# Moving the gate branch and the norm of q into the channel tiles of a recurrence

## The chip, the cores and the metric

The kernel runs on one core of a Trainium2 chip, in one launch. The metric is the device time of one execution in microseconds. The kernel before takes 1188.15 us, the median of three runs (1186.73 to 1192.13).

## What is computed

One layer of a diffusion backbone: 1024 latent tokens with a context of 256, 1024 channels, float32. Of the reference, cut to what matters here (`x` and `ctx` are normed and modulated into `h` and `hc` first):

```
q, k, v, xr, gr = split(h @ w_in)          # q 512 columns, k 128, v 128, xr 512, gr 512
q = apply_rope_2d(rmsnorm(q, q_norm_g))    # per head of 64, 8 heads
k = apply_rope_2d(rmsnorm(k, k_norm_g))    # 2 heads
attn = windowed_attention_with_context(q, k, v, k_c, v_c, sink)
xc = centred_depthwise_conv(xr)            # width 4; context and latents apart
for d in (forward, backward):              # RG-LRU, 512 channels
    r = sigmoid(block_diag(xc, w_r[d]));  i = sigmoid(block_diag(xc, w_i[d]))
    log_a = -8 * r * softplus(-lam[d]);   a = exp(log_a)
    h_sum += scan(a, sqrt(-expm1(2 * log_a)) * i * xc)
y = concat([attn, h_sum * gelu(gr)]) @ w_out
x = x + g1 * y
x = x + g2 * expert_choice_moe(modulate(rmsnorm(x)))    # 16 experts, SwiGLU, 128 tokens each
```

## The kernel before

All products with large weights are done in float32r in three parts: a float32 weight or activation is split into a high half (`whi`, `hh`) by a copy on ScalarE and a low half (`wlo`, `hl`) by a subtraction on VectorE, and a product is high x high + high x low + low x high. A weight of 256 columns is fetched by SyncE into one of two raw buffers (`load_raw`, `win`), and `split_w` makes the halves (L241 on ScalarE, L243 on VectorE); three of each can be held.

The part that the change touches lies between the keys and values and the attention, 175 to 326 us:

- **Recurrence** (`lru_tile`, channel tiles t = 3, 2, 1, 0 of 128 channels; 1280 time steps in a row). TensorE multiplies the convolved input with two gates in two directions (`pgatec` for the context, `pgate` for the latents). ScalarE makes tanh of the four, then `a` = exp and one more tanh for each direction, then two square roots. VectorE multiplies `i` with the input (L503), the factor with the root (L507, L508), scans both directions (L511, L513, L515) and adds them into `xr` (L517).
- **Projection of q** (`proj`, `pproj`): 2 groups g of 256 columns by 8 blocks b of 128 tokens, 24 matmuls each; ScalarE copies each into `QB[b]`. Five of these 16 steps stand behind each of the first three tiles and one behind the last.
- **Gate branch**, behind all four tiles: for each channel tile 48 matmuls (`pgr`), gelu on ScalarE (`ge`), and the product with `xr` on VectorE (L585).
- **Keys** (`k_stack`): each pair of key heads is copied twice, transposed on TensorE, and split into `kh` and `kl`.
- **Norm and rotation of q** (`norm_rope`), behind the gate branch: squares on ScalarE (L404), sums on VectorE (L406), the reciprocal root on GpSimd (`rstd_of`, L147 and L149), then on VectorE the product with it (L408), two cross terms (L418), the cosine term (L420) and the sum (L421). It needs both groups of a block.
- **Attention** follows: `q_stack` transposes and splits a block of q (`qst`), `scores` multiplies it with the keys, `load_wout` splits the eight halves of the output weight (`woh`, `wol`), `oproj` is the output projection (`py`).

PSUM has two buffers of 1024 columns (tag S: gates, `pgr`, scores), one each of O0 and O1 (512 columns: `pproj` and `pgatec` in turn) and two for transposes (T). The framework that builds the program does not keep the written order: it makes one list of instructions for each engine ahead of time, from the dependencies and its own estimates, and each engine then runs its list strictly in order, waiting where an input is late or a buffer is not free. `act` is the exception: activations that go through it keep their written order among themselves (`tc.issue_after`, which orders an instruction behind another). ScalarE holds one set of functions at a time; a change of set is an ACT_TABLE_LOAD in its list. Exp and tanh share a set, sqrt has another, gelu another, which holds tanh as well: in the lists no load stands between gelu and a tanh that follows it.

Of the kernel before, what the change touches and what calls it, by code (L numbers as in the profile page):

```python
# [13 lines left out]
OP = mybir.AluOpType  # L14
# [34 lines left out]
def _body(tc, nc, A, out, dbg, top):  # L49
# [35 lines left out]
    def act(*a, **kw):  # L85
        """an activation whose table set matters: these keep their order on the engine"""
        if last_act[0] is None:
            i = nc.scalar.activation(*a, **kw)
        else:
            with tc.issue_after(last_act[0].ins):  # L90
                i = nc.scalar.activation(*a, **kw)  # L91
        last_act[0] = i
        return i
# [4 lines left out]
    def warm(n, after=None):  # L98
        """keeps the tensor engine's clock up while it waits"""
        p = pS("warm")  # L100
        for _ in range(n):
            with tc.issue_after(after.ins) if after is not None else nullcontext():
                after = nc.tensor.matmul(p[:, 0:128], ident, ident, start=True, stop=True)

# [47 lines left out]
    # softplus(-lam) = max(-lam, 0) + log1p(exp(-|lam|)); log1p(e) = 2 atanh(e / (2 + e))  # L152
# [22 lines left out]
    # sigmoid(z + b) = (1 + tanh(z / 2 + b / 2)) / 2  # L175
# [18 lines left out]
    def ada_chunk(n):  # L194
        """[4 groups x (16 rows of c, 16 of c_ctx), 512] of columns n*512.., in SBUF"""
        po = pO("pada")
        for q in range(2):
            for half in range(2):
                w = paw.tile([128, 4, 256], F32, name="wada")
                c0 = n * 512 + q * 256  # L200
                nc.sync.dma_start(w, w_ada[half * 512:(half + 1) * 512, c0:c0 + 256].rearrange("(k p) c -> p k c", p=128))
                for j in range(4):
                    nc.tensor.matmul(po[32 * j:32 * j + 32, q * 256:(q + 1) * 256], cst[:, half * 4 + j, :], w[:, j, :],  # L203
                                     start=(half == 0), stop=(half == 1),
                                     skip_group_check=True, tile_position=(0, 32 * j))
        ev = paw.tile([128, 512], F32, name="adaev", bufs=1)
        nc.vector.tensor_copy(ev, po)
        return ev

    ada_ev = {}  # L210
    gcol = const.tile([128, 40], F32, name="gcol")       # g1, sh2, sc2, g2, (1 + sc2) * norm2_g

    def ada_col(n):
        """half of one of g1, sh2, sc2, g2 as columns; the half before is finished first"""
# [40 lines left out]
    def projT(hi, lo, segs):  # L255
        """channel rows: [128 channels, tokens]"""
        for k in range(KT):
            for w, which in ((hi, (0, 1)), (lo, (0,))):
                for i in which:
                    for o, sg in segs:  # L260
                        h, c0, n = SEG[sg][i], SEG[sg][2], SEG[sg][3]
                        mm(o, w[:, k, :], h[:, k, c0:c0 + n], k == 0 and w is hi and i == 0, k == KT - 1 and w is lo)

# [1 line left out]
    AB = const.tile([128, 2, 8, 2], F32, name="ab")      # (scale, shift), k tile, (lat, ctx)  # L265
    a0 = pool(S_a0, "a0", 2)
    a0x = pool(S_a0, "a0x", 6)
    xT = a0.tile([128, KT, 768], F32, name="xT", bufs=1)      # [ctx 256 | lat 512]
# [24 lines left out]
    def ada_half(h):  # L293
        """scale and shift of half of the channels"""
# [64 lines left out]
    XR14 = pxr.tile([128, 4, NT + 6], F32, name="xr")    # slots 1 to 4; slot 0  # L359
    XR0 = pxr.tile([128, NT + 6], F32, name="xr0")  # L360
    XR = [XR0] + [XR14[:, i] for i in range(4)]
    XC0, XL0 = 0, NCTX + 3                               # [2 | ctx | 1 | 2 | lat | 1]
# [9 lines left out]
    def rope_tables(nm, after=None):  # L372
        """weights of the norm; cos and sin tables with them folded in"""
# [16 lines left out]
    def proj(wg, tt):  # L390
        """token rows: [128 tokens, 256 columns]"""
# [9 lines left out]
    def norm_rope(x, nh, b, tabs_):  # L401
        """x: [128, nh, 64], in place; b: latent block, or None (no rope)"""
# [54 lines left out]
    def gate_weights(t):  # L457
        """block-diagonal [128, (gate, direction), 128] of the channel tile"""
# [8 lines left out]
    def conv(t):  # L467
        """into slot t + 1, whose input is used up"""
# [62 lines left out]
    # the router with the second norm's scale in its rows, and its shift's share as a row  # L531
# [13 lines left out]
    qsteps = [(g, b) for g in range(2) for b in range(NB)]  # L545
    for i, t in enumerate((3, 2, 1, 0)):
        lru_tile(t)
        for g, b in qsteps[5 * i:5 * i + 5]:
            if b == 0:
                wg = split_group(load_raw(g * 256))  # L550
            po = proj(wg, b + 2)
            nc.scalar.activation(QB[b][:, g * 256:(g + 1) * 256], po, AF.Copy)

    S_lru.close()

# [20 lines left out]
    with tc.tile_pool(name="grt", bufs=2, side="right", reuse_waits="tile") as pg_:  # L576
        for t in (3, 2, 1, 0):
            if t % 2:
                raw = load_raw(1280 + (t - 1) * 128)
            w0 = xr_weights(raw, t)  # L580
            lat = pS("pgr")
            projT(w0[0], w0[1], [(lat[:, 0:512], LAT0), (lat[:, 512:1024], LAT1)])
            ge = pg_.tile([128, S], F32, name="ge")
            act(ge, lat, AF.Gelu_apprx_tanh)
            nc.vector.tensor_tensor(XR[t + 1][:, 0:S], XR[t + 1][:, 0:S], ge, op=OP.mult)  # L585
            if t in (1, 0):
                k_stack(1 - t)
        for b in range(NB):
            norm_rope(QB[b].rearrange("p (h d) -> p h d", h=8), 8, b, qtab)
    tiny = const.tile([128, 1], F32, name="tiny")  # L590
    act(tiny, nsink[:, 0:1], AF.Exp)
# [15 lines left out]
    S_wo, S_wr, S_cs, S_att = (ExitStack() for _ in range(4))  # L607
    WO = []                                              # (hi, lo) of the attention's rows, of the recurrence's rows
# [27 lines left out]
    def q_stack(b):  # L636
        """[128 (hi, lo), head, 128]; heads 2i: (hi, lo), heads 2i + 1: (lo, hi)"""
# [11 lines left out]
    def scores(b, kv, i, qst):  # L649
        """heads kv * 4 + i and kv * 4 + 2 + i of 128 queries: negated scores, then their exponentials"""  # L650
# [5 lines left out]
        # keys: the window, then the context; for the last block the other way round  # L656
# [38 lines left out]
    def attn_out(b, kv, i, pe, ktiles, mx):  # L695
# [20 lines left out]
        # [(head pair, d), (head of the pair, query)]  # L716
        nc.scalar.activation(QB[b][:, kv * 256 + i * 128:kv * 256 + (i + 1) * 128], po, AF.Copy)

    y7 = QBQ[1].rearrange("p a b -> p (a b)")[:, 0:D]         # the last block's share of the recurrence, over queries used up

    def oproj(b, hh, part):
        """half of the columns of x + g1 * (mixed @ w_out); part 0: the recurrence's rows of w_out, 1: the attention's"""
# [95 lines left out]
    # ---- the 128 largest affinities of each expert: halves of blocks sorted on their own, then merged  # L818
# [3 lines left out]
    def resort(m, np_, steps=(64, 32, 16, 8, 4, 2, 1)):  # L822
        """bitonic rows sorted downwards"""
# [9 lines left out]
    def sort_blocks(b0, n):  # L833
        """n blocks from b0: rows (block, expert), sorted downwards"""
        q = n * 32
        f = 1 if n == 4 else 2                           # rows per block and expert
# [20 lines left out]
    def merge(a, b):  # L857
        """the 128 largest of two sorted rows: bitonic"""
# [29 lines left out]
    for u, (b, kv, i) in enumerate(units):  # L888
# [15 lines left out]
        if u == 3:  # L904
            XA = praw.tile([128, 2, D], F32, name="xa", tag="raw")     # residual stream of two blocks
            XB = praw.tile([128, 2, D], F32, name="xb", tag="raw")     # the same, normalised
            load_res(0)
            load_res(1)
# [28 lines left out]
    tri = prt.tile([128, 2, 128], BF, name="tri")        # tri[t', t] = t' <= t; ones  # L937
# [49 lines left out]
    POS = prt.tile([128, NB, NE], F32, name="pos")  # L987
    VAL = prt.tile([128, NB, NE, 4], BF, name="val")     # token row within its block, 3 parts of the affinity
    pd = pool(top, "moe", 2)
    # the threshold and how many of the ties at it are taken, as rows on every partition  # L990
# [3 lines left out]
    ge = rt.tile([128, NB, 2, NE], BF, name="ge")        # above the threshold; at it  # L994
# [13 lines left out]
    def prefix(m):  # L1008
        """inclusive count over the tokens before (block by block), per expert"""
# [43 lines left out]
    def load_chunk(key):  # L1053
        """the next 256 rows of a weight: per 128 of them what float32r holds, and the rest"""
# [44 lines left out]
    def split_x(src, first=False):  # L1099
        """the second norm's scale and shift on the way"""  # L1100
# [141 lines left out]
```

## Time and profile before

| | |
|---|---|
| median of three runs | 1188.15 us |
| the profiled execution, first to last instruction (span; all that the profile gives of its own time) | 1185.1 us |
| gates of tile 3 to the first score | 175.0 to 326.0 us |
| attention and what is between its blocks | 326 to about 575 us |
| experts | about 600 us to the end |
| TensorE, VectorE, ScalarE busy over the span | 92%, 80%, 67% |

The times of the profile count from the span's start. A busy time is what an engine spends in instructions; a matmul's record also covers its way through the array, so neighbouring records overlap, and the distance between two starts is the better measure of what one costs. The distance is also used for VectorE, whose records overlap by some 0.08 us. What ends an idle time is named behind the arrow.

### The profile page before, as it was taken

What the parts mean: (1) busy time and instruction counts of PE and PEld (TensorE: products, weight loads), DVE (VectorE), ACT (ScalarE), POOL (GpSimd) and SP (SyncE); (2) the same over time, 40 slices, a digit from 0 to 9 for tenths busy, and PEclk for the clock granted to TensorE, in tenths of its full rate; (3) what the DMA queues carried; (4) which work ended last, traced back from release to release, by engine and by line L of the source; (5) the groups of instructions that cost most, each with busy time, mean ns of one, the idle gap of its engine ahead of it and who ended that gap; (6) DMA issues with size and microseconds to landing.
All of it is one profiled execution on the core that took longest, in us unless ns stands there. A gap on an engine that the chain in (4) does not pass through costs nothing.

```text
span 1185.1 us, 17663 instructions
## 1 busy us (share of the span) xinstructions
PE 1091.7 (92%) x6481; PEld 876.0 (74%) x6481; DVE 946.1 (80%) x1577; ACT 792.2 (67%) x1159; POOL 148.6 (13%) x216
## 2 busy tenths in 40 slices
PE   3889999899799999999299999999999999999996
PEld 1568787667678888877187888888888888887774
DVE  3664557678795585867988999999999999989885
ACT  3652127666385666664268888888888888887873
POOL 2031110111300000000010111011111011110001
PEclk9999999899889999999699999999999999999998
DMA  9857720102141112116889999999999999999932
GB/s 293 293 175 239 236 64 5 40 1 69 37 108 54 55 54 89 55 54 235 334 300 342 342 382 399 382 391 388 384 381 402 383 394 380 383 377 355 359 101 36
DMA packets 97678, 277.14 MB, mean 234 GB/s; under 512 B 6060, under 2 KB 38088, under 8 KB 97592
## 3 DMA queue, kind: packets, MB, share of 16 engines
q1 hardware_dynamic: 90944, 255.87, 57.7%
q0 software_dynamic: 6000, 20.01, 6.8%
q8 instruction: 51, 0.84, 0.3%
q14 instruction: 35, 0.29, 0.1%
q10 hardware_dynamic: 648, 0.13, 0.1%
HBM read 259.21 MB, written 16.79 MB: 233 GB/s over the span
## 4 chain that ended last, share of the span: by engine, by line
PE 68%; DVE 12%; issue 7%; ACT 7%; DMA 4%; POOL 1%; SPq 0%; POOLq 0%; ACTq 0%; DVEq 0%
PE pu L96 14%; PE pg L96 14%; PE pd L96 13%; PE py L96 7%; PE pxr L96 3%; PE pav L713 3%; PE pscore L96 3%; PE pPT L703 3%; DVE mlo L1066 2%; DMA wada<-in_w_ada_dram 2%; ACT gate L91 2%; PE pproj L96 1%; PE pada L203 1%; PE pT L1107 1%; DVE gate L507 1%
## 5 line engine op out<-in xcount | busy, mean ns | idle before, releaser
L1066 DVE TENSOR_TENSOR mlo<-mraw,mhi 128x1024 fp32r<-128x1024 f32 x384 | 448.1, 1217 | 24.5 <-ACT mhi L1063 23.1
L1063 ACT ACTIVATE mhi<-mraw 128x1024 fp32r<-128x1024 f32 x384 | 397.7, 1064 | 75.4 <-PE pg L96 29.0
L96 PE MATMUL pg<-mlo,xsh 128*128 128x512 f32 x256 | 81.9, 401 | 1.4 <-DVE mlo L1066 1.4
L96 PE MATMUL pg<-mhi,xsh 128*128 128x512 f32 x256 | 80.9, 397 | 0.4 <-ACT xsh L1117 0.3
L96 PE MATMUL pu<-mlo,xsh 128*128 128x512 f32 x256 | 80.2, 394 | 0.8 <-DVE mlo L1066 0.5
L96 PE MATMUL pu<-mhi,xsh 128*128 128x512 f32 x256 | 80.8, 390 | 0.0
L96 PE MATMUL pg<-mhi,xsl 128*128 128x512 f32 x256 | 80.4, 395 | 0.0
L96 PE MATMUL pu<-mhi,xsl 128*128 128x512 f32 x256 | 79.1, 390 | 0.0
L96 PE MATMUL pd<-mlo,hdh 128*128 128x512 f32 x240 | 76.0, 398 | 2.4 <-DVE mlo L1066 2.4
L96 PE MATMUL pd<-mhi,hdh 128*128 128x512 f32 x240 | 76.3, 399 | 0.0
L96 PE MATMUL pd<-mhi,hdl 128*128 128x512 f32 x240 | 74.2, 390 | 0.0
L1156 POOL DMA_INDIRECT out_dram<-ys,idx x16 | 49.8, 3113 | 164.2 <-DVE ys L1154 164.2
L1094 POOL DMA_INDIRECT xs<-xh_dram,idx x16 | 21.4, 1335 | 373.0 <-ACT mhi L1063 317.2
L1116 ACT ACTIVATE xs<-pT,gcol 128x128 f32<-128x128 f32 x124 | 46.9, 462 | 26.2 <-PE pT L1107 26.2
L91 ACT ACTIVATE sc<-sc,mx 128x641 f32<-128x641 f32 (+1 forms) x64 | 50.9, 798 | 15.7 <-DVE mx L677 15.7
L96 PE MATMUL pproj<-wlo,hh 128*128 128x256 f32 x192 | 55.5, 289 | 4.4 <-DVE wlo L243 4.4
L677 DVE CUSTOM_DVE_ANT_0 sc<-pscore,kn,nsink 128x640 f32<-128x640 f32 (+1 forms) x64 | 53.4, 842 | 6.0 <-PE pscore L96 5.8
L96 PE MATMUL pproj<-whi,hh 128*128 128x256 f32 x192 | 57.5, 300 | 0.6 <-ACT gate L91 0.6
L709 ACT ACTIVATE pt<-pPT 128x512 f32<-128x512 f32 (+1 forms) x88 | 44.0, 533 | 18.7 <-PE pPT L703 17.6
L96 PEld LDWEIGHTS pu<-mlo,xsh 128*128 128x128 f32 x256 | 47.1, 188 | 12.6 <-DVE mlo L1066 3.5
L96 PEld LDWEIGHTS pg<-mhi,xsl 128*128 128x128 f32 x256 | 48.6, 190 | 10.6
L96 PEld LDWEIGHTS pg<-mlo,xsh 128*128 128x128 f32 x256 | 46.2, 189 | 13.5 <-DVE mlo L1066 4.6
(329 smaller groups left out, 2444.7 us busy)
## 6 DMA issues: line engine op xcount, KB each, us to landing
mraw<-in_w_gate_dram SPq DMA_DIRECT2D x64, 1024.0 KB, 7.6
mraw<-in_w_up_dram SPq DMA_DIRECT2D x64, 1024.0 KB, 9.3
mraw<-in_w_down_dram SPq DMA_DIRECT2D x63, 1024.0 KB, 9.0
wada<-in_w_ada_dram SPq DMA_DIRECT2D x48, 512.0 KB, 5.8
win<-in_w_in_dram SPq DMA_DIRECT2D x7, 1024.0 KB, 5.4
xt<-in_x_dram SPq DMA_DIRECT2D x8, 512.0 KB, 4.3
xa<-in_x_dram SPq DMA_DIRECT2D x8, 512.0 KB, 3.8
out_dram<-xa SPq DMA_DIRECT2D x8, 512.0 KB, 2.7
```

Source lines behind the costliest of these rows:

```text
L91: i = nc.scalar.activation(*a, **kw)
L96: nc.tensor.matmul(o, l, r, start=start, stop=stop)
L203: nc.tensor.matmul(po[32 * j:32 * j + 32, q * 256:(q + 1) * 256], cst[:, half * 4 + j, :], w[:, j, :], start=(half == 0), stop=(half == 1) ...
L677: nc.vector.tensor_tensor_reduce(out=sb[:, :ntot], in0=ps[:, n0:n0 + ntot], in1=mk, scale=-0.125, scalar=nsink[:, h:h + 1], op0=OP.add, op ...
L703: nc.tensor.transpose(p[:, 2 * j + s, :], pe[s][:, (j0 + j) * 128:(j0 + j + 1) * 128], ident)
L709: nc.scalar.activation(dst, src, AF.Copy)
L713: nc.tensor.matmul(po[s * 64:(s + 1) * 64, :], V[:, kt, kv * 64:(kv + 1) * 64], pt[:, j, s], start=(j == 0), stop=(j == nk - 1), skip_grou ...
L1063: nc.scalar.activation(hi, raw[:, j], AF.Copy)
L1066: nc.vector.tensor_tensor(lo, raw[:, j], hi, op=OP.subtract)
L1094: g = nc.gpsimd.indirect_dma_start(out=xs, out_offset=None, in_=xh_dram, in_offset=bass.IndirectOffsetOnAxis(ap=idx[:, :1], axis=0))
L1116: nc.scalar.activation(xf[:, k], p[:, i], AF.Identity, scale=A_, bias=B_)
L1156: nc.gpsimd.indirect_dma_start(out=out_rows, out_offset=bass.IndirectOffsetOnAxis(ap=idx[:, :1], axis=0), in_=ys, in_offset=None, compute_ ...
```

## The change

The gate branch is moved into the loop over the channel tiles: behind each tile come its gate projection, its gelu, and the product with `xr`. The 16 q steps are divided 4, 4, 4, 4: group 0 behind tiles 3 and 2, group 1 behind tiles 1 and 0, and each block is normed and rotated right behind its second half. The gate weight of a pair of tiles is fetched behind tile 3 and tile 1, ahead of the q weight. `k_stack` for both pairs of heads comes behind the whole. `ge` has one buffer in the recurrence's pool instead of two in a pool of its own. (Comments and docstrings are also dropped; that is left out here.)

```diff
-    qsteps = [(g, b) for g in range(2) for b in range(NB)]
+    def gate_branch(t, raw):
+        w0 = xr_weights(raw, t)
+        lat = pS("pgr")
+        projT(w0[0], w0[1], [(lat[:, 0:512], LAT0), (lat[:, 512:1024], LAT1)])
+        ge = pl.tile([128, S], F32, name="ge")
+        act(ge, lat, AF.Gelu_apprx_tanh)
+        return ge
+
     for i, t in enumerate((3, 2, 1, 0)):
         lru_tile(t)
-        for g, b in qsteps[5 * i:5 * i + 5]:
+        if t % 2:
+            graw = load_raw(1280 + (t - 1) * 128)
+        ge = gate_branch(t, graw)
+        nc.vector.tensor_tensor(XR[t + 1][:, 0:S], XR[t + 1][:, 0:S], ge, op=OP.mult)
+        g = i // 2
+        for b in range(4 * (i % 2), 4 * (i % 2) + 4):
             if b == 0:
                 wg = split_group(load_raw(g * 256))
             po = proj(wg, b + 2)
             nc.scalar.activation(QB[b][:, g * 256:(g + 1) * 256], po, AF.Copy)
+            if g:
+                norm_rope(QB[b].rearrange("p (h d) -> p h d", h=8), 8, b, qtab)
+
+    tiny = const.tile([128, 1], F32, name="tiny")
+    act(tiny, nsink[:, 0:1], AF.Exp)
     S_lru.close()
...
-    with tc.tile_pool(name="grt", bufs=2, side="right", reuse_waits="tile") as pg_:
-        for t in (3, 2, 1, 0):
-            if t % 2:
-                raw = load_raw(1280 + (t - 1) * 128)
-            w0 = xr_weights(raw, t)
-            lat = pS("pgr")
-            projT(w0[0], w0[1], [(lat[:, 0:512], LAT0), (lat[:, 512:1024], LAT1)])
-            ge = pg_.tile([128, S], F32, name="ge")
-            act(ge, lat, AF.Gelu_apprx_tanh)
-            nc.vector.tensor_tensor(XR[t + 1][:, 0:S], XR[t + 1][:, 0:S], ge, op=OP.mult)
-            if t in (1, 0):
-                k_stack(1 - t)
-        for b in range(NB):
-            norm_rope(QB[b].rearrange("p (h d) -> p h d", h=8), 8, b, qtab)
-    tiny = const.tile([128, 1], F32, name="tiny")
-    act(tiny, nsink[:, 0:1], AF.Exp)
+    for kv in range(2):
+        k_stack(kv)
```

**ScalarE, tile 2, from its exp to the gates of tile 1.** Before (`a` is an exp, the `gate<-gate` ahead of the load a tanh, the two behind it square roots):

```order
L91 ACTIVATE a<-gate,sp 128x1280
L552 ACTIVATE qb<-pproj 128x256
L91 ACTIVATE gate<-gate,sp 128x1280
L91 ACT_TABLE_LOAD
L91 ACTIVATE gate<-gate 128x1280 x2
L552 ACTIVATE qb<-pproj 128x256 x2
L241 ACTIVATE whi<-win 128x1024 x2
L552 ACTIVATE qb<-pproj 128x256
L404 ACTIVATE nrsq<-qb 128x512
L552 ACTIVATE qb<-pproj 128x256
L91 ACT_TABLE_LOAD
L91 ACTIVATE gate<-pgatec,hb 128x256
```

After, from the last gate of tile 2 on:

```order
L91 ACTIVATE gate<-pgate,hb 128x1024
L91 ACT_TABLE_LOAD
L91 ACTIVATE a<-gate,sp 128x1280
L91 ACTIVATE gate<-gate,sp 128x1280
L91 ACTIVATE a<-gate,sp 128x1280
L91 ACTIVATE gate<-gate,sp 128x1280
L91 ACT_TABLE_LOAD
L91 ACTIVATE gate<-gate 128x1280 x2
L91 ACT_TABLE_LOAD
L91 ACTIVATE ge<-pgr 128x1024
L565 ACTIVATE qb<-pproj 128x256
L241 ACTIVATE whi<-win 128x1024
```

A load now stands ahead of the exp, and one for gelu behind the roots; the load ahead of the next gates is gone. Over the whole list 12 loads have become 15.

**VectorE, from the second gate product (L503) of tile 0 to its scan.** Before:

```order
L503 SCALAR_TENSOR_TENSOR gate<-gate,xr 128x1280
L418 TENSOR_TENSOR nrt_2697<-qb,rope 128x16x16
L420 TENSOR_TENSOR qb<-qb,rope 128x512
L243 TENSOR_TENSOR wlo<-win,whi 128x1024
L421 TENSOR_TENSOR qb<-qb,nrt_2697 128x512
L507 SCALAR_TENSOR_TENSOR gate<-a,gate 128x1280 x2
L508 TENSOR_TENSOR gate<-gate 128x1280 x2
L511 SCALAR_TENSOR_TENSOR gate<-a,gate 128x1280
L513 SCALAR_TENSOR_TENSOR gate<-a,gate 128x256
L243 TENSOR_TENSOR wlo<-win,whi 128x1024
L515 SCALAR_TENSOR_TENSOR gate<-a,gate 128x1024
L243 TENSOR_TENSOR wlo<-win,whi 128x1024
```

After:

```order
L503 SCALAR_TENSOR_TENSOR gate<-gate,xr 128x1280
L421 TENSOR_TENSOR qb<-qb,nrt_2396 128x512
L243 TENSOR_TENSOR wlo<-win,whi 128x1024
L418 TENSOR_TENSOR nrt_2436<-qb,rope 128x16x16 x2
L420 TENSOR_TENSOR qb<-qb,rope 128x512
L421 TENSOR_TENSOR qb<-qb,nrt_2436 128x512
L406 TENSOR_REDUCE nrss<-nrsq 128x8
L408 TENSOR_TENSOR qb<-qb,rs_2579 128x512
L418 TENSOR_TENSOR nrt_2582<-qb,rope 128x16x16 x2
L420 TENSOR_TENSOR qb<-qb,rope 128x512
L421 TENSOR_TENSOR qb<-qb,nrt_2582 128x512
L507 SCALAR_TENSOR_TENSOR gate<-a,gate 128x1280 x2
```

The last gate weight's low half (`wlo`, here of the gate branch, needed by TensorE for the projection behind tile 0) stands behind the second gate product and, further up, behind three norms. On TensorE four matmuls of that projection now stand ahead of 34 of q, and its other 44 behind those; in tiles 3 to 1 the list is 12 of gates, 48 of the gate projection, 96 of q.

**VectorE, the last rows ahead of the first q stack (`qst`).** Before:

```order
L421 TENSOR_TENSOR qb<-qb,nrt_2739 128x512
L418 TENSOR_TENSOR nrt_2753<-qb,rope 128x16x16 x2
L420 TENSOR_TENSOR qb<-qb,rope 128x512
L421 TENSOR_TENSOR qb<-qb,nrt_2753 128x512
L585 TENSOR_TENSOR xr<-xr,ge 128x1024
L572 TENSOR_TENSOR kl<-pT,kh 128x512 x2
L572 TENSOR_TENSOR kl<-pT,kh 128x256
L625 TENSOR_TENSOR wol<-woraw,woh 128x1024
L645 TENSOR_TENSOR qst<-pT,qst 64x4x128
L646 TENSOR_TENSOR qst<-pT,qst 64x4x128
```

After:

```order
L589 TENSOR_TENSOR kl<-pT,kh 128x256
L420 TENSOR_TENSOR qb<-qb,rope 128x512
L581 COPY xr_655<-kn 128x10x64
L421 TENSOR_TENSOR qb<-qb,nrt_2702 128x512
L581 COPY xr_655<-kn 128x10x64
L627 TENSOR_TENSOR wol<-woraw,woh 128x1024 x2
L589 TENSOR_TENSOR kl<-pT,kh 128x512 x2
L627 TENSOR_TENSOR wol<-woraw,woh 128x1024
L589 TENSOR_TENSOR kl<-pT,kh 128x256
L627 TENSOR_TENSOR wol<-woraw,woh 128x1024
L647 TENSOR_TENSOR qst<-pT,qst 64x4x128
L648 TENSOR_TENSOR qst<-pT,qst 64x4x128
```

The last norms, both halves of the second key pair and four halves of w_out (`wol`) now stand ahead of the q stack; before, the last product with the gelu (L585) and one half of w_out did.

## Rows read from the trace of the kernel before

**Rows 1.** The page's first lines: the span, and each engine's busy time (share) xinstructions.
```profile
span 1185.1 us, 17663 instructions
...
PE 1091.7 (92%) x6481; PEld 876.0 (74%) x6481; DVE 946.1 (80%) x1577; ACT 792.2 (67%) x1159; POOL 148.6 (13%) x216
```

**Rows 2.** A window (attention): us, PE, PEld, DVE, ACT, POOL busy (x), PEclk, DMA, GB/s.
```profile
365.00:560.00 195.00, 192.12 (x1488) 155.30 (x1487) 136.37 (x433) 120.96 (x279) 13.83 (x69) 1.00 0.23 86
```

**Rows 3.** TensorE's waits, 172 to 326 us: total us, times, longest us.
```profile
PE pproj L96 <- DVE wlo L243: 4.4, 1, 4.4
PE pT L569 <- DVE kl L572: 3.4, 1, 3.4
```

**Rows 4.** VectorE's waits, 172 to 326 us, same columns.
```profile
DVE gate L507 <- ACT gate L91: 18.6, 4, 6.9
DVE qb L408 <- POOL rs L149: 15.6, 8, 2.1
```

**Rows 5.** TensorE's timeline: start us, us, engine line op, out<-in, xcount [idle <-releaser].
```profile
175.02 0.68 PE L96 MATMUL pgatec<-xr,wg 128*128 128x256 f32 x2
...
183.31 0.68 PE L96 MATMUL pproj<-whi,hh 128*128 128x256 f32 x1
183.83 0.28 PE L96 MATMUL pproj<-wlo,hh 128*128 128x256 f32 x1
183.95 0.28 PE L96 MATMUL pproj<-whi,hl 128*128 128x256 f32 x1
...
314.87 0.61 PE L96 MATMUL pgr<-hl,whi 128*128 128x512 f32 x2
315.32 0.61 PE L96 MATMUL pgr<-hh,wlo 128*128 128x512 f32 x2
```

**Rows 6.** VectorE's timeline, the scans of tile 3: first and last of six.
```profile
193.44 2.89 DVE L507 SCALAR_TENSOR_TENSOR gate<-a,gate 128x1280 f32<-128x1280 f32 x2 [6.88 <-ACT gate L91]
...
204.87 1.23 DVE L517 TENSOR_TENSOR xr<-gate 128x1024 f32<-128x1024 f32 x1
```

**Rows 7.** ScalarE's timeline, tile 3: last gate, table load, square roots.
```profile
183.91 1.11 ACT L91 ACTIVATE gate<-pgate,hb 128x1024 f32<-128x1024 f32 x1 [0.67 <-PE pgate L96]
...
190.84 1.28 ACT L91 ACT_TABLE_LOAD   x1
192.13 2.43 ACT L91 ACTIVATE gate<-gate 128x1280 f32<-128x1280 f32 x2
```

**Rows 8.** VectorE's timeline, norm and rotation of q blocks.
```profile
309.82 0.68 DVE L406 TENSOR_REDUCE nrss<-nrsq 128x8 f32<-128x512 f32 x1
310.42 0.68 DVE L421 TENSOR_TENSOR qb<-qb,nrt 128x512 f32<-128x512 f32 x1
312.91 0.69 DVE L408 TENSOR_TENSOR qb<-qb,rs 128x512 f32<-128x512 f32 x1 [1.81 <-POOL rs L149]
313.52 0.75 DVE L418 TENSOR_TENSOR nrt<-qb,rope 128x256 f32<-128x256 f32 x2
314.31 0.69 DVE L420 TENSOR_TENSOR qb<-qb,rope 128x512 f32<-128x512 f32 x1
```

**Rows 9.** VectorE's timeline, a half of w_out and the q stack; TensorE's first score.
```profile
324.01 1.23 DVE L625 TENSOR_TENSOR wol<-woraw,woh 128x1024 fp32r<-128x1024 f32 x1 [0.52 <-ACT woh L624]
325.26 0.68 DVE L645 TENSOR_TENSOR qst<-pT,qst 64x512 fp32r<-64x512 f32 x1
...
326.00 0.58 PE L96 MATMUL pscore<-kh,qst 128*128 128x256 f32 x1 [2.37 <-DVE qst L645]
```

**Rows 10.** The same columns in two windows around TensorE's 4.4 us wait.
```profile
225.00:230.00 5.00, 1.35 (x6) 1.35 (x7) 5.00 (x4) 0.00 (x0) 0.00 (x0) 0.77 0.03 8
230.00:235.00 5.00, 5.00 (x22) 4.28 (x21) 3.71 (x4) 2.25 (x4) 1.11 (x2) 0.55 0.62 202
```

**Rows 11.** TensorE's waits, 326 to 365 us: second and last of six.
```profile
PE py L96 <- ACT mh L731: 0.5, 1, 0.5
...
PE pPT L703 <- ACT pt L709: 0.2, 1, 0.2
```


## The prediction, made before the run

> **What bounds the kernel now.** I read the page first, then the waits of TensorE and VectorE between 172 and 326 us, then those engines' timelines there. The span is 1185.1 us [rows 1]; the runs have a median of 1188.15 us, 3.05 more, and I add every difference to the median. From 365 to 560 us, in the attention, TensorE is busy for 192 of 195 us at full clock [rows 2]: whatever delays its start there delays the end, because nothing later has room to make it up. So the question is when the attention gets going, that is, when its first score matmul runs (326.00 us now) and how much other work is done by then.
>
> Before 326 us neither engine is full. TensorE waits once for 4.4 us for the low half of a q weight, and once for 3.4 us in the transposes of the keys [rows 3]. VectorE waits 18.6 us for the scan's coefficients from ScalarE and 15.6 us for the reciprocal roots that GpSimd computes for the norm of q [rows 4]. TensorE's last gate projection ends at 315.9 us [rows 5], the first score starts 10 us later: between them stands VectorE's queue. So the reader is to see two engines that take turns, and a last stretch that belongs to VectorE.
>
> **What the change moves.** No matmul and no vector operation is added or dropped; three table loads are, 12 become 15 in the order of ScalarE. The work of a channel tile is now closed: gates, gate projection, four q blocks. Step by step:
>
> *TensorE, tiles 3 to 1.* The gates take 8.3 us (175.02 to 183.31). A q block is 24 matmuls at 0.12 us, four blocks 11.5 us. The gate projection is 24 pairs at 0.45 us, 10.9 us [rows 5]. A tile is 30.7 us, and no wait stands in it as long as ScalarE and VectorE keep the order's pace; so gates start at 175.0, 205.7, 236.4 and 267.1 us. The halves of these weights are split in time. One load comes later: SyncE now fetches a gate weight where it fetched the first q weight, and the q weight behind it. That holds back ScalarE's copy of one tile's input and one convolution, into the 6.9 us that VectorE idles ahead of its first scan [rows 6]; I price it at nothing, and the whole delay, were it longer, would show as a later first scan.
>
> *ScalarE.* From the start of the gates to the first square root's end, which releases VectorE, tile 3 takes 18.4 us (193.44 - 175.02) [rows 5, 6]. In the other tiles a load for exp now stands behind the tanh of the gates: 1.29 us from its start to the next instruction's [rows 7]. With that, and without a copy that stood there (0.3 us), 19.4 us. The loads for gelu stand behind the root and hold nothing that is late. VectorE's chain of tile 1 so starts at 236.4 + 19.4 = 255.8 us.
>
> A rule against the change stands in the Trainium skill, ScalarE: Activation LUTs, section What ACT_TABLE_LOAD costs: a switch costs the load of 1283 ns and a drain of about 1380 ns. The load takes 1.28 us here too, but its row lists no idle time ahead of it, and the next instruction starts 0.01 us behind it, so no drain shows [rows 7]. With a drain tile 1's chain, and so the whole, would be an estimated 1.4 us later; I go by the rows.
>
> *VectorE from 255.8 us to the first keys' scores.* This is the term that decides. In its order now stand, one behind the other: two scan chains, 12.6 us each (193.44 to 204.87 plus 1.1) [rows 6]; the two products with the gelu, 1.1 each like the sum ahead of them; all eight norms, whose five steps take 3.3 us a block from start to start (0.60, 0.61, 0.79 for the two of the rotation's cross terms, and 0.69 and 0.68 less an overlap of 0.04) [rows 8]; two products with the gate i, 1.4 each (an estimate from its 1280 columns and the 1.1 of 1024 columns); one weight half, 1.1; six key halves and two key copies, 3.9 (estimates from the norm steps of the same 512 columns); four halves of w_out, 1.2 each (324.01 to 325.26) [rows 9], 4.6 with overlap. That is 25.1 + 2.3 + 26.4 + 2.8 + 1.1 + 3.9 + 4.6 = 66.2. To it come the waits for GpSimd: 15.6 us for the eight blocks now; from the sum of squares to the product with its root pass 3.1 us (309.82 to 312.91) [rows 8], less the sum itself and what the order puts behind it (0.6 to 1.4 us in most blocks); I take 11, between the two bounds: 15.6, no better covered than now, and 8, one microsecond a block. So the q stack comes at 255.8 + 77.2 = 333.0 us, and the first score 0.7 later, as now [rows 9]: 333.7 us, 7.7 us late.
>
> Where does this come from? Not from more work. VectorE idles between its second gate product and the scan in tiles 2 and 1: the product follows the last tanh, which ends 10.0 us after the gates' start (185.02 - 175.02) [rows 5, 7], and is done 11.5 us after it, the scan starts after 19.4, so 8 us each. Now it idles 6.9 there in tile 3, and the next tile's gates come sooner, since no gate projection stands ahead of them. It could have been rotating q there, but a q block is only complete when its second half is projected, and four of the eight are projected in tile 0, behind the last gates. So the half of the norms that remains falls behind the last scan, when TensorE has nothing left.
>
> *TensorE in tile 0.* The low half of the last gate weight stands on VectorE behind three norms and both gate products; it is done about 32.7 us into the sum, at 288.5 us. TensorE has run four matmuls of this projection and 34 of q by 280.2 and waits 8 us. Today a wait of 4.4 us lets the granted clock fall to 0.77 and 0.55 in the next two stretches of 5 us [rows 10], about 3 us lost; I take the same. The projection then ends at 301.5 us, the gelu at 302.6, and the squares of block 5 behind it at 305.7. VectorE wants them at about 307: 2 us of cover. Beyond that each lost microsecond counts.
>
> *What is given back.* At the first score four halves of w_out are done, against one now. VectorE so saves 3 x 1.2 = 3.5 us in the crowded opening of the attention: 7.7 - 3.5 = 4.2 us late. TensorE can gain less: in the opening it now waits 1.9 us in five waits behind the first score's own [rows 11], and it has three matmuls of the output projection behind it, 0.6 us: 7.7 - 2.5 = 5.2 us late. The later of the two holds: +5.2 us, 1193.4 us. The other engines give no other end: SyncE's list is the same but for the order of the w_in loads, and GpSimd's extra copies stand where its roots are not yet asked for.
>
> **The rivals.**
> (a) *TensorE sets the end of the stretch.* Its last projection ends at 301.5 + 62 x 0.12 = 309 us instead of 315.9, and the 4.4 us wait is gone. If the first score followed as it does now, 10 us later, all would be 6.9 us earlier: 1181.3 us. For it: 92% busy over the span [rows 1], and fewer waits in tiles 3 to 1. Against it: VectorE would have to be done at 319, 14 us before my sum. It decides once the tail of VectorE behind the last projection is shorter than 17 us; I have 24.
> (b) *The head start repays all.* With waits on GpSimd at the lower bound (8) the first score is at 330.7; the opening then gives back its 2.5 to 3.5, and 1.2 to 2.2 us stay: 1190 us. For it: VectorE has little idle time after 326.
> (c) *The cold clock joins.* The wait in tile 0 ends in a projection at half clock. If the clock stays down through its 44 matmuls (0.45 us a matmul instead of 0.23), 10 us are lost instead of 3, and 5 more reach the norms behind the 2 us of cover; with GpSimd's waits at 15.6, another 4.6: +5 to +15, 1201 us at the middle.
> That the change does not do what it says is excluded: the order shows the gelu in every tile.
>
> **How the numbers follow.** Forecast 0.50, with its own range +3 to +8.5 us; (a) 0.12; (b) 0.18; (c) 0.20. About 0.5%, 5.9 us, is what a measurement of this kernel can tell from no change. Of the forecast 0.22 lies above +5.9 us and 0.28 below; (c) lies above but for 0.01; (b) within; of (a) 0.01 within. So faster 0.11, same 0.48, slower 0.41. The range leaves out the better half of (a) and the worse part of (c): 1183 to 1202 us.
>
> **What would show it.** In the profile after: gates of the four tiles at 175, 206, 236 and 267 us; the first scan step of tile 1 at 256; a TensorE wait of 8 us on a low weight half near 280 with a fallen clock behind it; the last projection at about 309; the first score at 332 to 335, with a wait on VectorE ahead of it in place of one on TensorE's own work; four halves of w_out ahead of the q stack. I am wrong in the term that matters if VectorE reaches the q stack before 326 us, or if the attention from its second block on stands earlier than now although the first score is later.

## The result and the profile after

The changed kernel takes 1197.7 us (median of 6 runs, 1197.28 to 1198.57), the kernel before 1189.37 us beside it (6 runs, 1186.73 to 1192.13): ratio 1.0073, 95% interval 1.0057 to 1.0090. It is 8.3 us slower. The page of the changed kernel begins:

```profile
span 1196.5 us, 17647 instructions
...
PE 1090.5 (91%) x6481; PEld 875.5 (73%) x6481; DVE 945.6 (79%) x1577; ACT 799.5 (67%) x1162; POOL 151.1 (13%) x216
```

Against [rows 1] only ScalarE has clearly more to do (7.3 us), and GpSimd 2.5 us. In the attention's window, moved by 10 us, TensorE is as full as in [rows 2]:

```profile
375.00:570.00 195.00, 192.15 (x1489) 155.12 (x1488) 135.99 (x426) 121.33 (x278) 13.76 (x69) 1.00 0.23 83
```

So nothing was lost there; it came late. The profiled executions differ in their front too: the first gate starts at 176.37 us, against 175.02 in [rows 5], before anything is changed. Below I count from that first gate. Two rows mark the way: the first score, and the first matmul of the prefix sums of the routing, which follow the attention. Here is that row of the kernel before, and then both of the changed one (instructions, min/median/max ns, first and last start):

```profile
L96 PE MATMUL ppre<-ge,tri x36: 186/188/188, 585.1 to 586.0; 128*128 128x32 bf16 x36
```

```profile
L96 PE MATMUL pscore<-kh,qst x128: 277/334/580, 338.5 to 557.8; 128*128 128x256 f32 x80, 128*128 128x384 f32 x48
...
L96 PE MATMUL ppre<-ge,tri x36: 186/188/188, 596.2 to 597.1; 128*128 128x32 bf16 x36
```

The first score comes 162.1 us behind the first gate, where it was 151.0: 11.1 us late. The prefix comes 419.8 us behind it, where it was 410.1: 9.7 us late, so 1.4 us came back in the attention. Behind the prefix both have 600 us left.

TensorE's waits between 172 and 340 us (us, times, longest), to hold against [rows 3]:

```profile
PE py L96 <- ACT mh L733: 8.7, 1, 8.7
PE pgate L96 <- ACT gate L91: 5.2, 2, 3.4
PE pT L586 <- DVE kl L589: 4.9, 2, 4.5
PE pgr L96 <- DVE wlo L243: 4.4, 1, 4.4
PE pT L586 <- DVE xr L581: 3.6, 1, 3.6
PE pscore L96 <- DVE qst L647: 2.2, 1, 2.2
```

All six stand in tile 0 or behind it. Their places are in TensorE's timeline (start, us, engine line op, idle before it); the last row answers to the first score in [rows 9]:

```profile
176.37 0.68 PE L96 MATMUL pgatec<-xr,wg 128*128 128x256 f32 x2
...
277.81 0.70 PE L96 MATMUL pgate<-xr,wg 128*128 128x512 f32 x1 [3.40 <-ACT gate L91]
...
293.38 0.79 PE L96 MATMUL pgr<-hh,wlo 128*128 128x512 f32 x1 [4.36 <-DVE wlo L243]
...
312.14 0.28 PE L96 MATMUL pproj<-whi,hh 128*128 128x256 f32 x1
...
338.46 0.58 PE L96 MATMUL pscore<-kh,qst 128*128 128x256 f32 x1 [2.20 <-DVE qst L647]
```

From the last projection at 312 us to the first score, 26 us, TensorE's matmuls are busy for only about 7 us. Most of its waits there name VectorE. The longest, 8.7 us, names ScalarE's `mh`, but that stands behind a square that had itself waited 2.3 us for a sum on VectorE. VectorE's waits (compare [rows 4]) and its first and last step of the stretch that the prediction summed:

```profile
DVE gate L507 <- ACT gate L91: 23.2, 3, 8.2
DVE qb L408 <- POOL rs L149: 14.2, 8, 2.1
```

```profile
258.16 2.90 DVE L507 SCALAR_TENSOR_TENSOR gate<-a,gate 128x1280 f32<-128x1280 f32 x2 [8.21 <-ACT gate L91]
...
336.47 1.22 DVE L627 TENSOR_TENSOR wol<-woraw,woh 128x1024 fp32r<-128x1024 f32 x1
337.73 0.68 DVE L647 TENSOR_TENSOR qst<-pT,qst 64x512 fp32r<-64x512 f32 x1
```

From 258.16 us to the q stack the eight waits for roots are the only ones that VectorE's timeline lists. Its other idle time now lies ahead of the scans (8.2 us each in tiles 2 and 1), its work behind them. The windows between (columns of [rows 2]) show what the waits do to TensorE's clock, which is at its lower level, 1.2 GHz, from 320 us into the attention (in the kernel before it was so too, from 320 to 330 us):

```profile
310.00:320.00 10.00, 3.54 (x31) 3.30 (x29) 7.78 (x10) 4.85 (x9) 6.32 (x12) 0.86 0.00 0
320.00:330.00 10.00, 1.48 (x3) 0.58 (x3) 7.04 (x14) 2.55 (x4) 3.32 (x3) 0.50 0.00 0
330.00:340.00 10.00, 5.62 (x22) 4.43 (x23) 9.89 (x15) 2.77 (x5) 1.20 (x2) 0.50 0.63 170
340.00:350.00 10.00, 9.99 (x64) 8.64 (x64) 8.16 (x19) 7.50 (x17) 1.21 (x2) 0.77 0.69 150
```

### The profile page after: what moved, and what is told of

Read it like the earlier page. It is cut to its first block, busy times and chain, and to the rows that moved or that the text cites. A ratio compares the mean times of both kernels' runs of the same rounds, so it can differ in the third digit from the quotient of the medians.

```text
span 1196.5 us, 17647 instructions
## 1 busy us (share of the span) xinstructions
PE 1090.5 (91%) x6481; PEld 875.5 (73%) x6481; DVE 945.6 (79%) x1577; ACT 799.5 (67%) x1162; POOL 151.1 (13%) x216
## 4 chain that ended last, share of the span: by engine, by line
PE 71%; DVE 12%; issue 6%; DMA 5%; ACT 3%; POOL 2%; SPq 0%; POOLq 0%; ACTq 0%; DVEq 0%
PE pu L96 14%; PE pg L96 13%; PE pd L96 12%; PE py L96 7%; PE pxr L96 3%; PE pav L715 3%; PE pproj L96 3%; DMA wada<-in_w_ada_dram 3%; PE pscore L96 3%; PE pPT L705 3%; DVE mlo L1068 2%; PE pgr L96 2%; PE pgate L96 2%; POOL rs L149 1%; PE pada L203 1%
## 5 line engine op out<-in xcount | busy, mean ns | idle before, releaser
L96 PE MATMUL py<-woh,mh 128*128 128x512 f32 x128 | 54.9, 429 | 9.7 <-ACT mh L733 8.7
L679 DVE CUSTOM_DVE_ANT_0 sc<-pscore,kn,nsink 128x640 f32<-128x640 f32 (+1 forms) x64 | 53.5, 844 | 10.8 <-PE pscore L96 10.5
L96 PEld LDWEIGHTS pg<-mhi,xsl 128*128 128x128 f32 x256 | 48.5, 190 | 10.6
L96 PEld LDWEIGHTS pu<-mhi,xsh 128*128 128x128 f32 x256 | 48.0, 188 | 10.4 <-ACT mhi L1065 0.3
L96 PEld LDWEIGHTS pu<-mhi,xsl 128*128 128x128 f32 x256 | 48.1, 188 | 10.2
```

The lines of the kernel that those rows point to most:

```text
L96: nc.tensor.matmul(o, l, r, start=start, stop=stop)
L679: nc.vector.tensor_tensor_reduce(out=sb[:, :ntot], in0=ps[:, n0:n0 + ntot], in1=mk, scale=-0.125, scalar=nsink[:, h:h + 1], op0=OP.add, op ...
```

## Experiments

Theory: VectorE's row from the first scan of tile 1 to the q stack sets when the attention starts; half of q's norms can only stand behind the last projections, and each waits for a root from GpSimd. Rivals: the table loads; TensorE's own list with its waits; the place of the norms as such. Two parts of the changed order stay in all that follows, and no run tests them by themselves: both key pairs behind the tiles, and how many halves of w_out stand ahead of the q stack.

All runs in one table. The last three columns are worked out from the same rows' first starts: first gate to first score, first score to prefix, and their sum, in us of the profiled execution. Times are medians; beside the experiments the kernel before measured 1187.9 to 1188.5, beside the changed kernel itself 1189.4.

| run | us | ratio to before (95%) | gate to score | score to prefix | sum |
|---|---|---|---|---|---|
| before | 1189.4 | | 151.0 | 259.1 | 410.1 |
| changed | 1197.7 | 1.0073 (1.0057 to 1.0090) | 162.1 | 257.7 | 419.8 |
| changed again (e12) | 1197.9 | 1.0075 (1.0060 to 1.0090) | 162.0 | 256.9 | 418.9 |
| e1 gate branch alone | 1196.0 | 1.0053 (1.0033 to 1.0072) | 160.1 | 256.5 | 416.6 |
| e2 norms and dealing alone | 1207.0 | 1.0146 (1.0126 to 1.0166) | 167.0 | 260.9 | 427.9 |
| e8 dealing alone | 1192.7 | 1.0039 (1.0026 to 1.0052) | 156.7 | 258.6 | 415.3 |
| e3 changed, factor last | 1186.1 | 0.9984 (0.9973 to 0.9996) | 148.0 | 260.6 | 408.6 |
| e4 before, factor last | 1188.5 | 0.9999 (0.9990 to 1.0009) | 150.7 | 258.6 | 409.3 |
| e5 changed, no gelu | 1198.9 | 1.0083 (1.0064 to 1.0101) | 163.4 | 256.6 | 420.0 |
| e6 changed, half blocks | 1200.5 | 1.0092 (1.0071 to 1.0114) | 161.9 | 259.0 | 420.9 |
| e7 half blocks, factor last | 1185.5 | 0.9972 (0.9957 to 0.9988) | 146.0 | 263.2 | 409.2 |
| e9 extra work in the gap | 1196.8 | 1.0070 (1.0054 to 1.0086) | 162.1 | 257.5 | 419.6 |
| e10 extra work in the tail | 1206.9 | 1.0161 (1.0140 to 1.0182) | 166.6 | 262.0 | 428.6 |
| e11 e1, factor last | 1186.8 | 0.9989 (0.9976 to 1.0002) | 147.8 | 260.7 | 408.5 |

### Is it VectorE's row? Extra work at two places

Four useless sums, once in VectorE's gap ahead of the scan of tile 2 (e9), once behind the last norm (e10).

```diff
+    def extra(after):
+        for _ in range(4):
+            with tc.issue_after(after.ins):
+                after = nc.vector.tensor_reduce(extra_o, Kn, axis=AX.X, op=OP.add)
...
+        if t == 2:              # e9: behind the second product with xc
+            extra(last)
...
+    extra(last)                 # e10: behind the last norm_rope instead
```

> The changed kernel with four more sums on VectorE (128x1280 each, about 1.6 us, an estimate from the 0.68 us of the 128x512 sum), into a tile that nothing reads, between the last product with the channel rows and the scan's first product in tile 2, where VectorE sat idle for 8.2 us. Theory (that idle time is no part of the path, TensorE sets the tile's period there): no change from the changed kernel, 1196 to 1199 us. Rival (the scan's row of every tile is the path): 1202 us and more.

> The same four sums in the changed kernel, pinned behind the last norm of q, ahead of the first block's stack. Theory (VectorE's row up to the stack is the path): their some 6 us appear in the time nearly whole, less what attention gives back: 1201 to 1204 us. Rival (what stands between the norms and the scores is TensorE's or ScalarE's): 1196 to 1199 us.

> The changed kernel once more beside these: 1196 to 1199 us, as before; it is what the others of this set are held against.

In the gap they cost nothing (1196.8 against 1197.9 us). VectorE's timeline of e9 shows why: the 6 us are taken out of the idle time, 2.2 are left.

```profile
217.63 6.04 DVE L484 TENSOR_REDUCE extra<-kn 128x10 f32<-128x1280 f32 x4
225.91 2.89 DVE L516 SCALAR_TENSOR_TENSOR gate<-a,gate 128x1280 f32<-128x1280 f32 x2 [2.24 <-ACT gate L91]
```

In the tail the same sums (5.9 us busy) cost 9.0 us, more than expected. The first score is 4.5 us later, and the attention gives back 4.3 less. One half of w_out (1.2 us) now stands behind the q stack instead of ahead of it, so VectorE's row up to the stack grew by less than the sums. From 340 to 350 us the clock is at 0.50 in e10, where the changed kernel had 0.77, and the DMA engines, with the loads of w_out, at 0.98 instead of 0.69:

```profile
340.00:350.00 10.00, 7.54 (x30) 6.69 (x31) 8.61 (x19) 5.88 (x14) 0.00 (x0) 0.50 0.98 228
```

How the 4.3 us divide among the clock, the loads and the half that the attention now has to do, these runs don't tell. (The mask, written over the keys that the sums read, also waited 2.9 us on GpSimd.) What the theory needs is plain all the same: the work is free at one place and delays the first score at the other.

### The waits for the roots

A norm's factor is one number for each head, so it can be multiplied in behind the rotation, when the root has long come. No instruction is added. e3 does so in the changed kernel, e4 in the kernel before, e11 in e1.

```diff
-        nc.vector.tensor_tensor(x, x, rs[:, :, None].to_broadcast([128, nh, 64]), op=OP.mult)
+        if nh == 2:
+            nc.vector.tensor_tensor(x, x, rs[:, :, None].to_broadcast([128, nh, 64]), op=OP.mult)
...
         nc.vector.tensor_tensor(x, x, t2, op=OP.add)
+        if nh > 2:
+            nc.vector.tensor_tensor(x, x, rs[:, :, None].to_broadcast([128, nh, 64]), op=OP.mult)
```

> The changed kernel with the norm's factor (GpSimd's root) multiplied in behind the rotation instead of ahead of it: the same instructions, but VectorE has three more of a block to do (2.2 us) before it needs the root, and little of the 14.2 us that it waited for the eight roots should be left. Theory (VectorE's row sets the end): the first score falls from 338.5 to 327-331 us, where TensorE's own list stands next, and the time by 6 to 10 us, to 1188 to 1192 us. Rivals (table loads, TensorE's clock): the roots lie beside other work, 1196 to 1199 us.

> The kernel before with the norm's factor multiplied in behind the rotation. Its TensorE list binds up to the last gate projection (315.9 us); from there to the first score (326.0) VectorE's norms are late. Theory: a few of those 10 us go, 1183 to 1187 us. Rival (there too TensorE's order is all, the 15.6 us of waits for roots lie beside it): 1187.5 to 1190 us.

> The gate branch in the tiles, the norms issued behind the loop, and the norm's factor behind the rotation. If the norms' place adds nothing once the roots are hidden: 1184 to 1188 us, as with the factor last alone. If the place of the norms helps by bringing half of them into tile 1 earlier: 1190 us and more.

e3 takes 11.6 us off by the medians (10.6 by the two ratios), more than expected, and is 2.4 us below the kernel before measured beside it. VectorE's wait for roots, 14.2 us, is down to this, and the first score stands at:

```profile
DVE qb L424 <- POOL rs L149: 0.3, 1, 0.3
```

```profile
324.49 0.58 PE L96 MATMUL pscore<-kh,qst 128*128 128x256 f32 x1 [2.00 <-DVE qst L650]
```

That is 14.1 us earlier behind the first gate; 2.9 us of it are lost again up to the prefix. The roots took 13.9 us less, but that the two figures are so near is partly luck. Ahead of the q stack VectorE now has two halves of w_out, not four (2.3 us less, left to the attention), and it waits 2.3 us for ScalarE at the scan of tile 0, where it had not waited:

```profile
291.08 2.89 DVE L510 SCALAR_TENSOR_TENSOR gate<-a,gate 128x1280 f32<-128x1280 f32 x2 [2.27 <-ACT gate L91]
...
317.70 1.22 DVE L630 TENSOR_TENSOR wol<-woraw,woh 128x1024 fp32r<-128x1024 f32 x1
...
322.18 1.21 DVE L630 TENSOR_TENSOR wol<-woraw,woh 128x1024 fp32r<-128x1024 f32 x1
```

The waits in tile 1 counted like those in the tail: from the scan of tile 1 to that of tile 0 VectorE took 42.9 us in the changed kernel (258.16 to 301.02) and 32.8 in e3, and from there to the q stack 36.7 and 32.7 (the steps of one block moved from the first stretch to the second). With them went TensorE's wait of 4.4 us for the weight half.

In the kernel before, the same edit buys nothing (e4: ratio 0.9999): the waits for roots fell from 15.6 us to 5.4, and the first score came 150.7 us behind the first gate instead of 151.0. That expectation was a miss. Two shifts cancel here. The first score does follow the last gate matmul sooner, 7.3 us behind its start instead of 10.5. But that matmul itself starts 143.4 us behind the first gate instead of 140.5: in e4's order TensorE waits longer for a gelu (2.0 us in the kernel before), and its clock is at 0.91 instead of 1.00 from 290 to 310 us. VectorE is done early and then waits for the last gelu, that is for TensorE. The waits in e4:

```profile
PE pgr L96 <- ACT ge L91: 4.3, 1, 4.3
```

```profile
DVE xr L588 <- ACT ge L91: 8.2, 1, 8.2
DVE qb L424 <- POOL rs L149: 5.4, 4, 1.5
```

So with most of the roots hidden, TensorE's list is what binds in the old order, while in the changed order VectorE's row with its roots does. What the roots would be worth in the old order if TensorE's list had not moved, e4 does not show.

### One part of the change at a time

e1 takes the norms out of the loop again; e8 only deals q's blocks 4, 4, 4, 4 in the kernel before; e2 also issues each norm behind its block.

```diff
 e1, against the changed kernel
-            if g:
-                norm_rope(QB[b].rearrange("p (h d) -> p h d", h=8), 8, b, qtab)
...
+    for b in range(NB):
+        norm_rope(QB[b].rearrange("p (h d) -> p h d", h=8), 8, b, qtab)
     tiny = const.tile([128, 1], F32, name="tiny")
 e8, against the kernel before
-        for g, b in qsteps[5 * i:5 * i + 5]:
+        for g, b in qsteps[4 * i:4 * i + 4]:
 e2: e8, the norms behind the gate branch dropped, and in the loop
+            if g:
+                norm_rope(QB[b].rearrange("p (h d) -> p h d", h=8), 8, b, qtab)
```

> The gate branch stays in the channel tiles, the eight norms of q are issued behind the tiles again. Theory (VectorE's row behind the first scan of tile 1 sets the end: scans, eight norms of 3.6 us, their waits on GpSimd's roots, the last split of weights): the row holds the same work, so the time stays at that of the changed kernel, 1196 to 1199 us. Rival (the place of the norms costs: their squares on ScalarE stand before gates of tile 0, and TensorE waited 3.4 and 1.8 us for those gates): the squares stand elsewhere now, and the time falls to 1190 to 1193 us.

> The kernel before with the blocks of q dealt 4, 4, 4, 4 to the tiles and nothing else: the gate branch and the norms stay behind the tiles. If the 18 us of the run with the dealing and the norms moved come from the dealing (each tile has one block, 2.9 us of TensorE's work, less to cover the gates' way through ScalarE and VectorE, and the clock falls in the waits): 1202 to 1208 us. If they come from the norms' place: 1187 to 1191 us.

> The kernel before with the blocks of q dealt 4, 4, 4, 4 to the channel tiles and each norm issued behind its block; the gate branch stays behind the tiles. Theory: the last norms lie beside 44 us of gate projections on TensorE, as before; 1186 to 1192 us, no change from the kernel before. Rival (moving the norms into the tiles is what costs, by roots or by squares between the gates): 1195 to 1199 us.

e1 keeps nearly all of the loss (1196.0 us). The order on VectorE is made by what is ready, so the norms go to nearly the same places from behind the loop; with the factor last the two are alike (e11 1186.8, e3 1186.1). The place of the norms in the code costs some 0 to 2.5 us. e1 and e11 both came out as first expected.

e2 was expected at no change, by the rival at 1195 to 1199, and is 18.5 us slower than the kernel before, the most of all runs but e10. Two things add up. TensorE's waits in e8, then in e2:

```profile
PE pgatec L96 <- ACT gate L91: 10.9, 3, 3.9
```

```profile
PE pgatec L96 <- ACT gate L91: 10.6, 3, 3.9
PE pgr L96 <- DVE wlo L243: 8.8, 1, 8.8
```

With four blocks to a tile TensorE has 2.9 us less to do while ScalarE and VectorE work through the gates, and waits at the next gates (2.4 us in three waits in the kernel before). That costs 4.5 us (e8, between the two ranges expected for it). The other 14 come with the norms: they stand ahead of the weights of the gate projections on VectorE, whose low halves come from 299.8 us on instead of 286.2 (e8):

```profile
L243 DVE TENSOR_TENSOR wlo<-win,whi x3: 1206/1215/1218, 299.8 to 319.5; 128x1024 fp32r<-128x1024 f32 x3
```

Of the 14 us the wait of 8.8 is seen; how the rest arises was not followed up. So in the change the two parts lean on each other: the gate projection in the tile covers what four blocks alone do not, and its weights come ahead of the norms. Neither part alone is better than the kernel before.

### The table loads

e5 leaves the gelu out and puts tanh in its place.

```diff
-        act(ge, lat, AF.Gelu_apprx_tanh)
+        act(ge, lat, AF.Tanh)
```

> The changed kernel with tanh in gelu's place (gelu is left out; tanh is in the table set that the gates use): no table loads for the gate branch. Theory: the loads cost only what stands before the scan, one of 1.3 us in tile 1, and ScalarE has slack elsewhere: 1195 to 1198 us. Rival (table loads set the loss: two for each gelu and the change back, each 1.28 us and perhaps as long again for a drain that the row does not show): 1188 to 1193 us.

With 11 loads instead of 15 the time is the same (1198.9 us, 0.9 above the theory's range, far from the rival's). At the scan of tile 1 the load does show: it starts at 256.36 us instead of 258.16, which is 1.4 us earlier counted from the first gate; one load of 1.28 us and no drain. It is gone before the first score (163.4 against 162.1 us): in e5's order of tile 0 TensorE waits 5.5 us for the weight half and VectorE 3.3 us for a square, so the comparison is not clean from there on. e3 closes the gap from the other side: it has as many loads as the changed kernel and none of its loss, so the loads don't make that loss.

### Half blocks

```diff
-            if g:
-                norm_rope(QB[b].rearrange("p (h d) -> p h d", h=8), 8, b, qtab)
+            norm_rope(QB[b][:, g * 256:(g + 1) * 256].rearrange("p (h d) -> p h d", h=4), 4, b, qtab)
```

> The changed kernel with the norm taken of half a block (four heads) behind each projection, so that half of the norms come in tiles 3 and 2. A half costs about 2.2 us on VectorE (half-size rows by 0.42 and 0.25 us, an estimate from the 512 and 256 wide rows), a whole 3.6. Theory (VectorE's row behind the first scan of tile 1 sets the end): that row loses 8 x 1.4 = 11 us of work, TensorE's list stands next; 1187 to 1192 us. Rival (VectorE has no room in tiles 3 and 2: the low parts of the weights come late, TensorE waits there and its clock falls): 1196 to 1202 us.

> The norm of half blocks and the factor behind the rotation, both in the changed kernel. Theory: VectorE's row loses the waits for roots (11.6 us of the time in the run with the factor last alone) and 11 us of work; TensorE's own list, whose last projection of q came at 302 us there, is then what stands: 1178 to 1184 us. Rival (no room on VectorE in tiles 3 and 2): 1186 to 1192 us.

e6 is not faster than the change (1200.5 us): the theory's number was wrong. The rival's was right, but not its reason, for TensorE waits for no low half in e6. It waits 9.2 us in six waits for ScalarE at the gates, where squares stand that wait for VectorE's sums. Half of the norms do lie in tiles 3 and 2, but with twice the roots. VectorE's wait for them and its scans' starts in e6:

```profile
DVE qb L408 <- POOL rs L149: 18.6, 16, 1.2
```

```profile
195.87 2.89 DVE L507 SCALAR_TENSOR_TENSOR gate<-a,gate 128x1280 f32<-128x1280 f32 x2 [6.77 <-ACT gate L91]
231.20 2.90 DVE L507 SCALAR_TENSOR_TENSOR gate<-a,gate 128x1280 f32<-128x1280 f32 x2 [5.03 <-ACT gate L91]
265.85 2.90 DVE L507 SCALAR_TENSOR_TENSOR gate<-a,gate 128x1280 f32<-128x1280 f32 x2 [2.96 <-ACT gate L91]
```

A tile takes 35.3 and 34.7 us here, where TensorE's work in one is 31. So the scan of tile 1 came later (6.5 us) by what the rest got shorter (6.7). With the roots hidden as well (e7) the first score is the earliest of all (146.0), but the attention loses it again (263.2): 1185.5 us, between the two ranges expected, not told apart from e3 by the intervals, and 0.28% below the kernel before (interval 0.12% to 0.43%). It has the lowest median of all; that the stretch behind the first score then binds is read from the table, not tested further.

## Why the prediction came out as it did

It gave 1193.4 us, 5.2 over the 1188.15 then known. The measured difference of 8.3 us is inside the whole range and just under the top of the forecast's own (+3 to +8.5); 1197.7 us as such lies 1.0 us above that, because the kernel before came out slower too. The mechanism held, the size came out at its edge. Step by step, in us of the profile counted from the first gate:

- *TensorE, tiles 3 to 1.* 30.7 us a tile forecast, 31.0 measured (gates at 176.4, 207.5, 238.5, 269.5). The scan of tile 1 is 1.0 late against the forecast 255.8: 258.16 less the front's 1.35.
- *The load for exp.* Forecast at 1.29 us ahead of the scan; e5 shows 1.4. The Trainium skill (ScalarE: Activation LUTs, What ACT_TABLE_LOAD costs) adds a drain of about 1380 ns to a switch. Neither ScalarE's rows of the changed kernel, where the root starts 0.02 us behind the load, nor e5 shows one:

```profile
255.56 1.28 ACT L91 ACT_TABLE_LOAD   x1
256.86 2.44 ACT L91 ACTIVATE gate<-gate 128x1280 f32<-128x1280 f32 x2
```

- *VectorE's row.* 77.2 us forecast, 79.6 measured (258.16 to 337.73). Its work was 65.4 against 66.2. **The mis-sized term is the wait for GpSimd's roots: 14.2 us, where 11 was taken between bounds of 8 and 15.6.** Seven of the eight blocks wait 1.5 to 1.8 us and one 2.1, because VectorE's list mostly has only one or two steps of 0.6 to 0.8 us between a block's sum of squares and the product with its root. e3 shows that most of this was on the path: 10.6 to 11.6 us of the time.
- *TensorE in tile 0.* One wait of 8 us for a weight half was forecast near 280. It was 3.4 and 1.8 us for ScalarE at the gates and then 4.4 for the weight half at 293. ScalarE was held because the squares have one tile, and the next square waited for VectorE's sum, ahead of the gate that TensorE needed:

```profile
276.12 0.63 ACT L404 ACTIVATE nrsq<-qb 128x512 f32<-128x512 f32 x1 [5.50 <-DVE nrss L406]
```

  The 44 matmuls behind the last wait took 11.7 us instead of 10, so the fallen clock cost 1.7 us there, not 3. (The first window of [rows 10], from which the 3 were taken, holds the wait itself, which ends at 228.65 us.) The last projection came at 312.7 (311.3 net) against 309. This did not reach VectorE's row, which waited for nothing but the roots.
- *What is given back.* 2.5 us forecast, 1.4 measured, with four halves of w_out ahead of the stack as forecast.

The three misses, 1.0 + 2.4 + 1.1, make the 4.5 us between the forecast 5.2 and the 9.7 of the profile; the medians differ by 8.3.

Of the rivals, (a) is out: TensorE's last projection was 4.6 us earlier than [rows 5] net of the front, and the score did not follow it. (b) is out: the roots took 14.2 us, not 8, and too little came back. (c) had the right kind of surcharge in the roots, 3.2 of its 4.6 us; its 5 us by a cold clock in tile 0 did not come. Its +5 to +15 us hold the measured time as well, so the time alone does not decide between it and the forecast; the clock does. (Its 1201 us is the middle of +10 to +15, that of +5 to +15 is 1198.) What the prediction did not see is how near the better kernel lay: it took the wait for the roots as a price and did not ask whether it has to stand there. In the kernel before, the answer would have bought nothing (e4).

## What to carry to other kernels

When a change fills the engine that seemed to be the bound, look at what is late on the next one: here the projections got covered and the norms got uncovered, and waits for roots whose hiding bought nothing in the kernel before came to cost 10.6 to 11.6 us. Before pricing a wait for a slow engine, ask whether what is done with its answer can stand later: one factor for a whole head can be multiplied in before or after a rotation. And the price of a microsecond depends on its place: 5.9 us of the same work cost 0 in a gap and 9 behind it. To tell one place from the other, put useless work there and measure.

## What the hardware showed beside that

- The root of 8 numbers on each partition takes GpSimd two instructions, 0.49 and 1.64 us, 2.2 us from the start of the first to the end of the second (GpSimd's timeline of the changed kernel):

```profile
319.19 0.49 POOL L147 TENSOR_SCALAR rs_r<-nrss 128x8 f32<-128x8 f32 x1 [0.36 <-DVE nrss L406]
319.77 1.64 POOL L149 TENSOR_TENSOR rs<-rs_r,neghalf 128x8 f32<-128x8 f32 x1
```

- The attention starts at half clock in both kernels. In the changed one the granted clock is 0.50 from 320 to 340 us and 0.77 in the next ten, with the first score at 338.5. In the kernel before, with the first score at 326.0:

```profile
325.00:330.00 5.00, 3.47 (x13) 3.08 (x14) 4.87 (x9) 4.71 (x8) 0.00 (x0) 0.50 0.14 30
330.00:335.00 5.00, 5.00 (x34) 4.55 (x34) 4.53 (x11) 2.51 (x7) 0.31 (x2) 0.65 0.75 179
```

  So half clock there is not what the late start adds. In e10, with the first score at 341.7, it lasts longer, up to 350 us; why, these runs don't show.
